# Attention sinks moved into the score bank, head halves summed by loads, two weight sums in one operation

## The chip, the cores and the metric

One core of a Trainium2 chip runs the kernel. The metric is device time in microseconds (us). A smaller number is better. PE is the matrix engine, PEld its weight loads, DVE the vector engine, ACT the activation engine, POOL the general engine, SP the engine that only issues transfers.

## What is computed

One layer of a block with two branches, on a sequence of 2048 positions and 1024 channels, in float32:

```python
h = rms_norm(x, norm_g)
v_c, b_c, c_c, z_c, q, k, v, z_a, gate_logits = split(h @ w_in)
y_a = ((b_c * causal_conv3(c_c * v_c)) * silu(z_c)) @ w_conv_out
o   = sliding_window_attention(rms_norm(q), rms_norm(k), v, sinks) * silu(z_a)
y_b = o @ w_attn_out
merged = sigmoid(g_a) * y_a + sigmoid(g_b) * y_b
out = x + merged @ w_out
```

The attention has 16 query heads and 4 key heads of 64 channels, blocks of 128 queries and a window of 128 keys. Each head has a learned sink, a score that has no value behind it:

```python
m = maximum(max(scores, axis=-1), sink)
p = exp(scores - m)
p = p / (sum(p, axis=-1) + exp(sink - m))
```

## The kernel before

The sequence is worked in two tiles of T = 1024 positions. Nearly all matrix work is a fast form of block multiplication: seven products in place of eight for each pair of column blocks, the "units" of `sunit`, with float32 numbers split into a high and a low part (three matmuls of 128 x 512 for each chunk). A unit of weights `w..._raw` is loaded whole, four sums of its blocks are formed on DVE (`pieces_of`, `sums`), and ACT and DVE split blocks and sums into high (`_ah`, `_sh`, `_th`, `_d`) and low parts. The products gather in the PSUM banks `X`, `V` and `Y`; ACT copies between them (`Y<-X...`, L658).

The program is a list of steps ("ticks"). Each tick is one product of 12 matmuls on PE, about 2.7 us. `run` takes one product, and then all that tables of numbers have put at this tick (`put(n, f)`): forming weights, normalizing, attention. The order in which the Python code writes instructions is the order on each engine; each engine runs its list strictly in that order, except that transfers run beside it once issued. `vec` is DVE with a list of small chains (`Woven`): after each of its operations one waiting step of a chain is written.

Attention is cut into 64 blocks: tile t, key head j, block b of 128 queries, with 4 heads each. `attention` puts the stages of a block at ticks around its step n:

- n - 5: loads of queries and keys (SP)
- n: scores, `att_scores`. Six matmuls fill the one score buffer `s` (`ps_s`, two PSUM banks, 2 x 2 heads of 256 columns of which 192 are used): for each half h one of 384 columns (`s<-lows,kq`, L1236) and two of 192 (`s<-kq,q`, L1240). Then on DVE the mask, the maximum, and the small operations on `st` (128 x 4) for the maximum with the sink. `rq` holds the query factors, which are applied as the scale of the exponential
- n + 1: `att_exp`. ACT takes the exponential of the sink (L1262) and of the four heads (L1265), with their sums
- n + 2: `att_norm` and `att_flip` on DVE (`p<-p,st`, `f<-p`), and the store of `f` by POOL
- n + 4, 9, 10: the way back through memory (`x<-fd`), and the high and low parts `xh`, `xl`, `yp`, cut to the window by POOL
- n + 13: `att_values`, six matmuls of 256 columns into `po`
- n + 14, 15: `att_out`, two copies on ACT that bring one half of `po` to the other 64 partitions, and `att_sum`, two additions on DVE, then the store to `od`

When a tile's units for q, conv, gates are done, the units z and za follow. In `fin_z` the attention result `od` is loaded again (`zain<-od`, four loads a unit, SP) and multiplied by the gate `zas` on DVE. These products become the operands of the output projection.

Three parts of the order matter below. The first: `att_exp` ends at tick n + 1 and steps are at least 3 ticks apart, so the buffer `s` stands free in the tick n - 1. The second: ACT's list holds, beside attention, the copies of `Y` and `s5` and the casts of weight parts that need DVE's sums. The third: POOL's queue holds the transfers with an addition, among them `mt<-tha` (L1551), which add into memory.

Of the kernel before, what the change touches and what calls it, by code (L numbers as in the profile page):

```python
# [82 lines left out]
Z_AHEAD = (7, 4)  # L83
SUM_WAIT = 5
VALUES_LATER = ((0, 10), (0, 30))
EARLY_LOADS = ((0, 29), (0, 30), (0, 31))
# [39 lines left out]
def block_kernel(  # L126
# [22 lines left out]
    upool = ctx.enter_context(tc.tile_pool(name="upool", bufs=2))  # L149
    small = ctx.enter_context(tc.tile_pool(name="small", bufs=12))  # L150
    ps_x = ctx.enter_context(tc.tile_pool(name="ps_x", bufs=2, space=bass.MemoryType.PSUM))
# [66 lines left out]
    sink_r = cols[:, C_S:NC].rearrange("p (j h c) -> p j h c", h=2, c=2)  # L218
    nsink_r = consts.tile([P, NKV, 2, 2], F32, name="nsink_r")
    gqk = consts.tile([P, 1], F32, name="gqk")  # L220
# [7 lines left out]
    def prep_cols():  # L228
        nc.vector.tensor_scalar(
            out=gqk, in0=cols[:, C_Q : C_Q + 1], scalar1=cols[:, C_K : C_K + 1],  # L230
            scalar2=HD ** -0.5, op0=ALU.mult, op1=ALU.mult)
        nc.vector.tensor_scalar(
            out=hbias, in0=cols[:, C_B:C_Q], scalar1=0.5, scalar2=None, op0=ALU.mult)
        nc.vector.tensor_scalar(
            out=nsink_r, in0=sink_r, scalar1=-1.0, scalar2=None, op0=ALU.mult)

# [223 lines left out]
    def pieces_of(n):  # L460
# [37 lines left out]
        if kind in "SP":  # L498
# [508 lines left out]

    rqs = {}

# [13 lines left out]
    def fin_q(t, j):  # L1023
# [58 lines left out]
        def by_query(r):  # L1082

            rq = consts.tile([P, 2, HB, 2, 2], F32, tag="rq", bufs=4, name=f"rq{t}_{j}")
            if not by_pe:
                vec.tensor_copy(rq, r.rearrange("p (c q b h) -> p q b h c", c=2, q=2, h=2))
                rqs[t, j] = rq
# [5 lines left out]
            rqs[t, j] = rq  # L1093

# [131 lines left out]

    def att_scores(t, j, b, ld):
# [4 lines left out]
        sp = ps_s.tile([P, 2, 2, 2 * P], F32, tag="s", name=f"s{nm}")  # L1232
        for h in range(2):
            skip = (2 - h) * HD if first else 0
            keys = slice(h * HD + skip, (h + 3) * HD)
            nc.tensor.matmul(  # L1236
                sp[:, h, :, skip : 3 * HD], lhsT=kq[:, 1, h * P : (h + 1) * P], rhs=kz[:, :, keys],
                start=True, stop=False)
            for c in range(2):
                nc.tensor.matmul(  # L1240
                    sp[:, h, c, skip : 3 * HD], lhsT=q2[:, h, c, :], rhs=kq[:, 0, keys],
                    start=False, stop=c == 1)
        sg = sp.rearrange("p h c k -> p (h c) k")
# [5 lines left out]
        else:  # L1249
            vec.copy_predicated(sg[:, :, 2 * HD : 3 * HD], m, sg[:, :, 0:HD])  # L1250
        st = small.tile([P, 6, G], F32, tag="st", name=f"st{nm}")
        vec.tensor_reduce(out=st[:, 0], in_=sg[:, :, HD : 3 * HD], axis=AX.X, op=ALU.max)
        mul(st[:, 5].rearrange("p (h c) -> p h c", c=2), st[:, 0].rearrange("p (h c) -> p h c", c=2), rv)
        vec.scalar_tensor_tensor(
            out=st[:, 1], in0=st[:, 5], scalar=-1.0, in1=nsink_r[:, j].rearrange("p h c -> p (h c)"),
            op0=ALU.mult, op1=ALU.min)
        add(st[:, 2], sink_r[:, j].rearrange("p h c -> p (h c)"), st[:, 1])
        return sg, st, rv

    def att_exp(t, j, b, got):  # L1260
        sg, st, rv = got
        nc.scalar.activation(out=st[:, 3], in_=st[:, 2], func=AF.Exp)  # L1262
        p = slot([P, G, P], F32, f"p{t}_{j}_{b}")
        for i in range(G):
            nc.scalar.activation(  # L1265
                out=p[:, i, :], in_=sg[:, i, HD : 3 * HD], func=AF.Exp, bias=st[:, 1, i : i + 1],
                scale=rv[:, i // 2, i % 2 : i % 2 + 1], accum_out=st[:, 4, i : i + 1])
        return p, st
# [66 lines left out]
    def att_out(t, j, b, po):  # L1335
        pov = po.rearrange("p (h e s c q) -> p h e s c q", h=2, e=2, s=2, c=2)
        o = slot([P, 2, P], F32, f"o{t}_{j}_{b}")
        parts = []
        for e in range(2):
            own, oth = HALVES[e], HALVES[1 - e]  # L1340
            ov = o[own].rearrange("p c (h s q) -> p h s c q", h=2, s=2)
            nc.scalar.copy(ov, pov[oth, :, e])  # L1342
            parts.append((ov, pov[own, :, e]))
        return o, parts
# [77 lines left out]
    def fin_z(t, j, src, nm, use):  # L1422
        other = {}

        def load():
            for i, q in ((0, 0), (1, 1), (0, 1), (1, 0)):
                o = slot([P, H], F32, f"{nm}in{t}_{j}_{i}_{q}")
                nc.sync.dma_start(o, src[2 * j + i, :, hs(q)])
                other[i, q] = o

        def fin(i, q, val):
# [433 lines left out]
    def attention(t, places):  # L1865
        for r, n in enumerate(places):
# [19 lines left out]
            put(n + late + O_ + 1, step("z", lambda g, j=j, b=b: att_out(t, j, b, g["o"])))  # L1886
            put(n + late + S_, step("t", lambda g, j=j, b=b: att_sum(t, j, b, g["z"])))

# [55 lines left out]
    for t in range(NT):  # L1944
# [34 lines left out]

        zs = [("z", j) + fin_z(t, j, yd[t], "z", use_o) for j in range(NJ)]  # L1980
        zs += [("za", j) + fin_z(t, j, od[t], "za", use_y) for j in range(NJ)]
        zs[0][3]()
# [156 lines left out]
```

## Time and profile before

| | us |
|---|---|
| three runs | 1901.31, 1899.99, 1901.0 (median 1901.0) |
| the profiled execution, its time | 1900.13 |
| the profiled execution, its span | 1898.4 |
| busy PE, PEld | 1888.9, 1572.3 |
| busy DVE, ACT, POOL | 1547.3, 986.6, 590.5 |

The profile shows one execution. Its span, from the first to the last instruction, is 1.7 us less than its time. The granted TensorE clock is 1.0 throughout. A row of a group gives line, engine, operation, output and inputs, shape and count, then busy us and mean ns of one, then the engine's idle time just before and what ended it. A row of a timeline gives start in us, duration in us, engine, line, operation, names, and in brackets the idle time before it. DVE operations that go through the helper all stand at L278 and are told apart by their names. A matmul lasts longer in the profile (0.39 us for 512 columns) than the next one waits to start, since matmuls overlap; the distance of starts is what counts.

### The profile page before, as it was taken

What the parts mean: (1) busy time and instruction counts of PE and PEld (TensorE: products, weight loads), DVE (VectorE), ACT (ScalarE), POOL (GpSimd) and SP (SyncE); (2) the same over time, 40 slices, a digit from 0 to 9 for tenths busy, and PEclk for the clock granted to TensorE, in tenths of its full rate; (3) what the DMA queues carried; (4) which work ended last, traced back from release to release, by engine and by line L of the source; (5) the groups of instructions that cost most, each with busy time, mean ns of one, the idle gap of its engine ahead of it and who ended that gap; (6) DMA issues with size and microseconds to landing.
All of it is one profiled execution on the core that took longest, in us unless ns stands there. A gap on an engine that the chain in (4) does not pass through costs nothing.

```text
span 1898.4 us, 27426 instructions
## 1 busy us (share of the span) xinstructions
PE 1888.9 (100%) x8670; PEld 1572.3 (83%) x8670; DVE 1547.3 (82%) x2620; ACT 986.6 (52%) x1967; POOL 590.5 (31%) x846
## 2 busy tenths in 40 slices
PE   9999999999999999999999999999999999999999
PEld 7888888888888888888888888888888888888887
DVE  7988898898888767669799899888888777787754
ACT  7665455456666443434565545556666434444321
POOL 2073335335655000011462344445556000121000
PEclk9999999999999999999999999999999999999999
DMA  8286555558777857894584655567788887779653
GB/s 294 80 239 178 166 159 171 172 183 248 240 237 230 301 195 247 281 279 113 170 229 118 193 165 152 168 200 234 235 247 270 300 280 267 274 193 269 212 176 111
DMA packets 222497, 402.22 MB, mean 212 GB/s; under 512 B 30032, under 2 KB 104784, under 8 KB 212880
## 3 DMA queue, kind: packets, MB, share of 16 engines
q1 hardware_dynamic: 188224, 313.10, 50.4%
q0 software_dynamic: 30528, 78.94, 16.0%
q10 hardware_dynamic: 3600, 8.42, 1.3%
q8 instruction: 69, 1.13, 0.2%
q14 instruction: 76, 0.62, 0.1%
HBM read 271.09 MB, written 129.25 MB: 211 GB/s over the span
## 4 chain that ended last, share of the span: by engine, by line
PE 89%; DVE 5%; DMA 2%; ACT 2%; issue 1%; SPq 0%; POOL 0%; DVEq 0%; ACTq 0%; POOLq 0%
PE Y L640 33%; PE Xcv L640 4%; PE Vcv L640 4%; PE ya L1468 4%; PE Vq L640 2%; PE Xq L640 2%; PE Xyb L640 2%; PE Vyb L640 2%; PE Vo L640 2%; PE Xo L640 2%; PE Vza L640 2%; PE Xza L640 2%; PE po L1330 2%; PE Xgb L640 2%; PE Vgb L640 2%; PE Xga L640 2%
## 5 line engine op out<-in xcount | busy, mean ns | idle before, releaser
L1292 POOL DMA_DIRECT2D x<-fd x256 | 139.6, 552 | 128.8 <-DMA fd<-f 55.6
L1265 ACT ACTIVATE p<-s,st,rq 128x128 f32<-128x128 f32 x256 | 113.0, 450 | 0.1
L1313 POOL TENSOR_SCALAR_AFFINE_SELECT xh<-xh 64x512 fp32r<-64x512 f32 x64 | 59.3, 927 | 152.7 <-DVE xl L278 103.7
L1285 POOL DMA_DIRECT2D fd<-f x64 | 36.9, 577 | 209.4 <-DVE f L278 173.4
L1551 POOL DMA_DIRECT2D mt<-tha x16 | 13.8, 862 | 255.0 <-DVE tha L278 233.4
L640 PE MATMUL Xcv<-oph,wcv_ah 128*128 128x512 f32 x256 | 79.2, 390 | 0.0
L1313 POOL TENSOR_SCALAR_AFFINE_SELECT xl<-xl 64x512 fp32r<-64x512 f32 x64 | 66.2, 1034 | 4.4
L1313 POOL TENSOR_SCALAR_AFFINE_SELECT yp<-xl 64x512 fp32r<-64x512 f32 x64 | 58.2, 909 | 3.1
L1313 POOL TENSOR_SCALAR_AFFINE_SELECT yp<-yp 64x512 fp32r<-64x512 f32 x64 | 57.4, 898 | 4.2
L278 DVE SCALAR_TENSOR_TENSOR y<-u,cols,y 128x512 f32<-128x512 f32 x64 | 53.3, 834 | 3.8 <-ACT y L1379 2.7
L278 DVE TENSOR_TENSOR o<-po,o 64x256 f32<-64x256 f32 x128 | 53.4, 417 | 2.7 <-ACT o L1342 1.7
L640 PEld LDWEIGHTS Xcv<-oph,wcv_ah 128*128 128x128 f32 x256 | 47.6, 188 | 9.6
L278 DVE TENSOR_TENSOR p<-p,st 128x512 f32<-128x512 f32 x64 | 50.5, 790 | 3.3
L469 ACT CAST wcv_sh<-wcv_raw 128x1024 fp32r<-128x1024 f32 x16 | 16.8, 1051 | 69.7 <-DVE wcv_raw L278 69.7
L1265 ACT ACTIVATION_READ_ACCUMULATOR p<-s,st,rq 128x1 f32 x256 | 50.7, 198 | 0.0
L1342 ACT COPY o<-po 64x256 f32<-64x256 f32 x128 | 47.1, 368 | 6.2 <-DMA wpd_yb<-wph_yb 3.0
L1070 POOL DMA_DIRECT2D q2d<-q_h x64 | 44.2, 690 | 18.1 <-ACT q_h L1065 9.2
L640 PE MATMUL Xcv<-oph,wcv_al 128*128 128x512 f32 x128 | 49.8, 389 | 0.0
L2040 POOL DMA_DIRECT2D oc<-ocd x12 | 6.5, 543 | 136.0 <-DMA wyb_sh<-wpd_yb 119.7
L1070 POOL DMA_DIRECT2D q2d<-q_l x64 | 44.1, 689 | 13.7 <-DMA q2d<-q_h 5.0
L278 DVE TENSOR_TENSOR wcv_raw<-wcv_raw 128x512 f32<-128x512 f32 x64 | 47.3, 758 | 1.1
L278 DVE STREAM_TRANSPOSE f<-p 128x512 f32<-128x512 f32 x64 | 45.5, 711 | 2.9 <-DVE p L278 0.2
(713 smaller groups left out, 6457.9 us busy)
## 6 DMA issues: line engine op xcount, KB each, us to landing
gd<-th SPq DMA_DIRECT2D x64, 256.0 KB, 2.7
wcv_raw<-in_w_units SPq DMA_DIRECT2D x16, 1024.0 KB, 5.4
q<-q2d SPq DMA_DIRECT2D x64, 256.0 KB, 5.4
v<-vd SPq DMA_DIRECT2D x128, 128.0 KB, 3.5
fd<-f POOLq DMA_DIRECT2D x64, 256.0 KB, 4.4
x<-fd POOLq DMA_DIRECT2D x256, 64.0 KB, 3.2
th<-gd SPq DMA_DIRECT2D x48, 256.0 KB, 4.9
wga_raw<-in_w_units SPq DMA_DIRECT2D x8, 1024.0 KB, 5.3
```

The source lines that it names most:

```text
L278: r = f(*args, **kw)
L469: return (lambda: nc.scalar.copy(hi, src), lambda: vec.tensor_tensor(out=lo, in0=src, in1=hi.bitcast(F32), op=ALU.subtract))
L640: nc.tensor.matmul(ps, lhsT=w[:, j, :], rhs=b[:, m, :], start=start and j == 0 and i == 0, stop=j == KP - 1 and i == 2, skip_group_check=n ...
L1070: nc.gpsimd.dma_start(q2d[t][j][half, q * 2 * HB : (q + 1) * 2 * HB, i, e, :], src[HALVES[e]].bitcast(F32).rearrange("p (b x) -> p b x", x ...
L1265: nc.scalar.activation(out=p[:, i, :], in_=sg[:, i, HD : 3 * HD], func=AF.Exp, bias=st[:, 1, i : i + 1], scale=rv[:, i // 2, i % 2 : i % 2 ...
L1285: nc.gpsimd.dma_start(fd, f)
L1292: nc.gpsimd.dma_start(x[QUADS[k]], src[k])
L1313: nc.gpsimd.affine_select(out=d4, in_=s4, pattern=[[0, 2], [-32 * sg, 2], [0, G], [-sg, 32]], compare_op=ALU.is_gt if prev else ALU.is_ge, ...
L1330: nc.tensor.matmul(po[:, cs], lhsT=v2[:, kind + h, :], rhs=xx[:, :, h * HD : (h + 1) * HD], start=n == h == 0, stop=n == 2 and h == 1)
L1342: nc.scalar.copy(ov, pov[oth, :, e])
L1468: nc.tensor.matmul(ps, lhsT=w[:, j, cs], rhs=o[:, m, :], start=n == 0 and i == 0, stop=n == KC - 1 and i == 2)
L1551: nc.gpsimd.dma_start(mt[t][k, :, hs(q)], m, accum_op=ALU.add)
```

## The change

1. Sinks. `keep_query` divides the sinks by the query factors, once for a tile and key head (a reciprocal and a product on DVE, into the new `sr_` tiles). `att_bank` copies them at tick n - 1 on ACT into column 192 of the four heads in `s` (L1238 of the changed kernel). The maximum on DVE and the exponential on ACT then run over 129 columns in place of 128, so that the sink takes part in both. The separate exponential and three small DVE operations go.
2. Order of scores. For each half the two matmuls of 192 columns come first, and the one of 384 last.
3. Halves. `att_out` copies all 128 partitions of `po` with two operations; `att_store` stores the two halves of the partitions apart, into an `od` of twice the size (two transfers). The two DVE additions go. `fin_z` loads one half as before, and `LOW_AT` = 2 ticks later POOL issues a load of the other half that adds into the same tile.
4. Weight sums. The second pair of block sums is one DVE operation of 1024 columns in place of two of 512.
5. The pool of small tiles is smaller (`small` 12 to 10), which makes room for the wider tiles.

```diff
+LOW_AT = 2
...
-    od = [dram.tile([KC, P, T], F32, name=f"od{t}") for t in range(NT)]
+    od = [dram.tile([2, KC, P, T], F32, name=f"od{t}") for t in range(NT)]
...
-                        lambda: sub(raw[:, 1, 1], raw[:, 1, 1], raw[:, 0, 0]),
-                        lambda: sub(raw[:, 1, 0], raw[:, 1, 0], raw[:, 0, 0])))
+                        lambda: sub(raw[:, 1].rearrange("p h j c -> p h (j c)"),
+                                    raw[:, 1].rearrange("p h j c -> p h (j c)"),
+                                    raw[:, 0, 0].rearrange("p j c -> p (j c)").unsqueeze(1).to_broadcast(
+                                        [P, 2, H]))))
...
+        vec.reciprocal(out=s4, in_=rq.rearrange("p q b h c -> p (q b) (h c)"))
+        mul(s4, s4, sink_r[:, j].rearrange("p h c -> p (h c)").unsqueeze(1).to_broadcast([P, NB, G]))
...
+    def att_bank(t, j, b):
+        sp = ps_s.tile([P, 2, 2, 2 * P], F32, tag="s", name=f"s{t}_{j}_{b}")
+        nc.scalar.copy(sp[:, :, :, 3 * HD : 3 * HD + 1], sinks_of[t, j][:, b // HB, b % HB].unsqueeze(3))
+        return sp
...
-        vec.tensor_reduce(out=st[:, 0], in_=sg[:, :, HD : 3 * HD], axis=AX.X, op=ALU.max)
-        mul(st[:, 5].rearrange("p (h c) -> p h c", c=2), st[:, 0].rearrange("p (h c) -> p h c", c=2), rv)
+        vec.tensor_reduce(out=st[:, 0], in_=sg[:, :, HD : 3 * HD + 1], axis=AX.X, op=ALU.max)
         vec.scalar_tensor_tensor(
-            out=st[:, 1], in0=st[:, 5], scalar=-1.0, in1=nsink_r[:, j].rearrange("p h c -> p (h c)"),
-            op0=ALU.mult, op1=ALU.min)
-        add(st[:, 2], sink_r[:, j].rearrange("p h c -> p (h c)"), st[:, 1])
+            out=st[:, 1], in0=st[:, 0], scalar=-1.0, in1=rv.rearrange("p h c -> p (h c)"),
+            op0=ALU.mult, op1=ALU.mult)
...
-        nc.scalar.activation(out=st[:, 3], in_=st[:, 2], func=AF.Exp)
...
-        add(st[:, 5], st[:, 4], st[:, 3])
-        vec.reciprocal(out=st[:, 0], in_=st[:, 5])
+        vec.reciprocal(out=st[:, 0], in_=st[:, 2])
...
-    def att_sum(t, j, b, got):
-        o, parts = got
-        for ov, pv in parts:
-            add(ov, pv, ov)
-        nc.sync.dma_start(
-            od[t][2 * j : 2 * j + 2, :, b * P : (b + 1) * P].rearrange("c p q -> p c q"), o)
+    def att_store(t, j, b, o):
+        for l, half in enumerate(HALVES):
+            nc.sync.dma_start(
+                od[t][l, 2 * j : 2 * j + 2, :, b * P : (b + 1) * P].rearrange("c (e d) q -> d (c e) q", e=2),
+                o[half].rearrange("d c e q -> d (c e) q"))
...
+                if len(src) > 1:
+                    put(tick[0] + LOW_AT, lambda o=o, i=i, q=q: nc.gpsimd.dma_start(
+                        o, src[1][2 * j + i, :, hs(q)], accum_op=ALU.add))
...
-            put(n, step("s", lambda g, j=j, b=b: att_scores(t, j, b, g["l"])))
+            put(n - 1, step("k", lambda g, j=j, b=b: att_bank(t, j, b)))
+            put(n, step("s", lambda g, j=j, b=b: att_scores(t, j, b, g["l"], g["k"])))
```

The first place is ACT's list before the scores of block 7 of the last key head of tile 0 (`s_3_7`). The names `wz_1_...` are parts of a weight unit, `zs_...` gates, `o_`, `xh_`, `yp_` stages of earlier blocks. Before:

```order
L469 CAST wz_1_sh<-wz_1_raw 128x1024
L1342 COPY o_3_3_6174<-po_3_3_6136 64x4x2x32 x2
L1299 CAST xh_3_4_6177<-x_3_4_6002 128x512
L1300 CAST yp_3_4_6179<-x_3_4_6002 64x512
L1436 ACTIVATE zs_1_1_6134<-zs_1_1_6134 128x512
L1436 ACTIVATE zs_1_0_6195<-Y 128x512
L469 CAST wz_1_th<-wz_1_raw 128x1024
L658 COPY Y<-Xz_1_6229 128x512
```

The same place in the changed kernel:

```order
L467 CAST wz_1_sh<-wz_1_raw 128x1024
L1348 COPY o_3_3_6039<-po_3_3_6003 128x4x2x32 x2
L1308 CAST xh_3_4_6042<-x_3_4_5874 128x512
L1309 CAST yp_3_4_6044<-x_3_4_5874 64x512
L1443 ACTIVATE zs_1_1_6001<-zs_1_1_6001 128x512
L1443 ACTIVATE zs_1_0_6060<-Y 128x512
L467 CAST wz_1_th<-wz_1_raw 128x1024
L1238 COPY s_3_7_6081<-sinks_3_1925 128x4
L658 COPY Y<-Xz_1_6095 128x512
```

The sinks' copy stands behind the cast of `wz_1_th`, and the scores of this block wait for it.

The second place is PE's list at the same scores, between two products of the unit z. Before:

```order
L640 MATMUL Xz_1_6229<-oph_1_3_516,wz_1_al 128x512
L1236 MATMUL s_3_7_6245<-lows_148,kq_3_7_6049 128x2x192
L1240 MATMUL s_3_7_6245<-kq_3_7_6049,q_0_3_7_6047 128x192 x2
L1236 MATMUL s_3_7_6245<-lows_148,kq_3_7_6049 128x2x192
L1240 MATMUL s_3_7_6245<-kq_3_7_6049,q_0_3_7_6047 128x192 x2
L640 MATMUL Vz_1_6260<-oph_5_0_750,wz_1_sh 128x512 x2
```

In the changed kernel:

```order
L640 MATMUL Xz_1_6095<-oph_1_3_514,wz_1_al 128x512
L1250 MATMUL s_3_7_6081<-kq_3_7_5921,q_0_3_7_5919 128x192 x2
L1253 MATMUL s_3_7_6081<-lows_147,kq_3_7_5921 128x2x192
L1250 MATMUL s_3_7_6081<-kq_3_7_5921,q_0_3_7_5919 128x192 x2
L1253 MATMUL s_3_7_6081<-lows_147,kq_3_7_5921 128x2x192
L640 MATMUL Vz_1_6123<-oph_5_0_747,wz_1_sh 128x512 x2
```

The number of matmuls stays, and the group now begins with the narrow ones and ends with a wide one.

The third place is DVE's list at the normalization of the block before, `p_3_6`. Before:

```order
L278 TENSOR_TENSOR wz_1_al<-wz_1_raw,wz_1_ah 128x1024
L278 TENSOR_TENSOR o_3_2_6071<-po_3_2_6028,o_3_2_6071 64x4x2x32 x2
L278 TENSOR_TENSOR wz_1_d<-wz_1_raw,wz_1_d 128x512
L278 TENSOR_TENSOR zs_1_1_6134<-Y,s5z_0_6026 128x512
L278 TENSOR_TENSOR st_3_6_6082<-st_3_6_6082 128x4
L278 RECIPROCAL st_3_6_6082<-st_3_6_6082 128x4
L278 TENSOR_TENSOR p_3_6_6117<-p_3_6_6117,st_3_6_6082 128x512
L278 STREAM_TRANSPOSE f_3_6_6146<-p_3_6_6117 128x512
L278 TENSOR_TENSOR zin_0_0_0_5959<-zin_0_0_0_5959,zs_0_0_6100 128x512
L278 TENSOR_TENSOR wz_1_raw<-wz_1_raw 128x512 x4
```

In the changed kernel:

```order
L276 TENSOR_TENSOR wz_1_al<-wz_1_raw,wz_1_ah 128x1024
L276 TENSOR_TENSOR wz_1_d<-wz_1_raw,wz_1_d 128x512
L276 TENSOR_TENSOR zs_1_1_6001<-Y,s5z_0_5897 128x512
L276 RECIPROCAL st_3_6_5953<-st_3_6_5953 128x4
L276 TENSOR_TENSOR p_3_6_5984<-p_3_6_5984,st_3_6_5953 128x4x128
L276 STREAM_TRANSPOSE f_3_6_6012<-p_3_6_5984 128x512
L276 TENSOR_TENSOR zin_0_0_0_5832<-zin_0_0_0_5832,zs_0_0_5969 128x512
L276 TENSOR_TENSOR wz_1_raw<-wz_1_raw 128x512 x2
L276 TENSOR_TENSOR wz_1_raw<-wz_1_raw 128x1024
```

The additions into `o` and one small operation are gone ahead of the sums of `wz_1_raw`, and the last two sums have become one; the rest keeps its order.

More of the change, by code (lines that the diff above doesn't have):

```diff
@@ L149, in block_kernel @@
     upool = ctx.enter_context(tc.tile_pool(name="upool", bufs=2))
-    small = ctx.enter_context(tc.tile_pool(name="small", bufs=12))
+    small = ctx.enter_context(tc.tile_pool(name="small", bufs=10))
     ps_x = ctx.enter_context(tc.tile_pool(name="ps_x", bufs=2, space=bass.MemoryType.PSUM))
@@ L1006, in head_rms, with keep_query @@
         rsqrt(ms, 32, name, ss, 1.0 / HD, then)
-    rqs = {}
+    rqs, sinks_of = {}, {}
+    def keep_query(t, j, rq):
+        rqs[t, j] = rq
+        sr = sinks_of[t, j] = consts.tile(
+            [P, 2, HB, 2, 2], F32, tag="sr_", bufs=4, name=f"sinks{t}_{j}")
+        s4 = sr.rearrange("p q b h c -> p (q b) (h c)")
+        vec.reciprocal(out=s4, in_=rq.rearrange("p q b h c -> p (q b) (h c)"))
+        mul(s4, s4, sink_r[:, j].rearrange("p h c -> p (h c)").unsqueeze(1).to_broadcast([P, NB, G]))
     def squares_sum(a, name):
@@ L1086, in by_query @@
                 vec.tensor_copy(rq, r.rearrange("p (c q b h) -> p q b h c", c=2, q=2, h=2))
-                rqs[t, j] = rq
+                keep_query(t, j, rq)
                 return
@@ L1092, in by_query @@
                     vec.tensor_copy(rq[HALVES[e], :, :, h, :], rv[HALVES[h], :, :, :, e])
-            rqs[t, j] = rq
+            keep_query(t, j, rq)
         return fin
@@ L1231, in att_scores @@
         rv = rqs[t, j][:, b // HB, b % HB]
-        sp = ps_s.tile([P, 2, 2, 2 * P], F32, tag="s", name=f"s{nm}")
         for h in range(2):
@@ L1241, in att_scores @@
                     sp[:, h, c, skip : 3 * HD], lhsT=q2[:, h, c, :], rhs=kq[:, 0, keys],
-                    start=False, stop=c == 1)
+                    start=c == 0, stop=False)
+            nc.tensor.matmul(
+                sp[:, h, :, skip : 3 * HD], lhsT=kq[:, 1, h * P : (h + 1) * P], rhs=kz[:, :, keys],
+                start=False, stop=True)
         sg = sp.rearrange("p h c k -> p (h c) k")
@@ L1250, in att_scores @@
             vec.copy_predicated(sg[:, :, 2 * HD : 3 * HD], m, sg[:, :, 0:HD])
[L1251 to L1253 removed]
+        st = small.tile([P, 3, G], F32, tag="st", bufs=4, name=f"st{nm}")
+        vec.tensor_reduce(out=st[:, 0], in_=sg[:, :, HD : 3 * HD + 1], axis=AX.X, op=ALU.max)
         vec.scalar_tensor_tensor(
[L1255 to L1257 removed]
+            out=st[:, 1], in0=st[:, 0], scalar=-1.0, in1=rv.rearrange("p h c -> p (h c)"),
+            op0=ALU.mult, op1=ALU.mult)
         return sg, st, rv
@@ L1886, in attention @@
             put(n + late + O_ + 1, step("z", lambda g, j=j, b=b: att_out(t, j, b, g["o"])))
-            put(n + late + S_, step("t", lambda g, j=j, b=b: att_sum(t, j, b, g["z"])))
+            put(n + late + S_, step("t", lambda g, j=j, b=b: att_store(t, j, b, g["z"])))
     def next_tile(t, n0):
@@ L1978, in use_y @@
                 put(tick[0] + USE_WAIT[t], lambda: ca(B_AT[k % 2, q], k // 2)) if USE_WAIT[t] else ca(B_AT[k % 2, q], k // 2)
-        zs = [("z", j) + fin_z(t, j, yd[t], "z", use_o) for j in range(NJ)]
-        zs += [("za", j) + fin_z(t, j, od[t], "za", use_y) for j in range(NJ)]
+        zs = [("z", j) + fin_z(t, j, [yd[t]], "z", use_o) for j in range(NJ)]
+        zs += [("za", j) + fin_z(t, j, [od[t][0], od[t][1]], "za", use_y) for j in range(NJ)]
         zs[0][3]()
```

28 lines of the change are left out of this document (9 added, 19 removed).

## The prediction

> **What bounds the kernel now.** I read the page's busy times first, then PE's waits, then PE's starts in a quiet stretch.
>
> ```profile
> span 1898.4 us, 27426 instructions
> PE 1888.9 (100%) x8670; PEld 1572.3 (83%) x8670; DVE 1547.3 (82%) x2620; ACT 986.6 (52%) x1967; POOL 590.5 (31%) x846
> ```
>
> The reader is to see that PE is busy all the time and DVE four fifths of it. From the chain of waits between 715 and 735 us:
>
> ```profile
> 716.23 2.72 PE Vza L640 x12
> 718.95 2.72 PE Y L640 x12
> ```
>
> A product of 12 matmuls takes 2.72 us when nothing disturbs it, 0.227 us from start to start. PE's own waits, by what ended them:
>
> ```profile
> PE po L1330 <- POOL xl L1313: 0.9, 1, 0.9
> PE Y L640 <- DVE Vb L278: 0.4, 1, 0.4
> PE Y L640 <- DVE vr L278: 0.4, 2, 0.2
> ```
>
> Beside the opening, which the change leaves alone, these are the largest; PE hardly ever waits. So work taken from DVE pays only through waits of this size, and any new wait of PE is paid in full. The profiled execution took 1900.13 us, 1.7 over its span; the median of the runs is 0.9 above it. What a measurement of this kernel can tell from no change is about 0.2%, 3.8 us.
>
> **Work that leaves and arrives beside PE.** From the groups by line:
>
> ```profile
> L278 DVE TENSOR_TENSOR o<-po,o 64x256 f32<-64x256 f32 x128 | 53.4, 417 | 2.7 <-ACT o L1342 1.7
> L278 DVE TENSOR_TENSOR st<-cols,st 128x4 f32<-128x4 f32 x64 | 17.9, 280 | 2.2
> L278 DVE TENSOR_TENSOR st<-st,rq 128x4 f32<-128x4 f32 x64 | 15.9, 248 | 2.1
> L278 DVE TENSOR_TENSOR st<-st 128x4 f32<-128x4 f32 x64 | 13.6, 212 | 15.7 <-ACT p L1265 15.2
> L278 DVE TENSOR_TENSOR wcv_raw<-wcv_raw 128x512 f32<-128x512 f32 x64 | 47.3, 758 | 1.1
> L278 DVE TENSOR_TENSOR wcv_al<-wcv_raw,wcv_ah 128x1024 fp32r<-128x1024 f32 x16 | 19.4, 1213 | 0.1
> L1262 ACT ACTIVATE st<-st 128x4 f32<-128x4 f32 x64 | 13.2, 205 | 50.3 <-DVE st L278 49.6
> L1376 ACT COPY halo<-u 128x2 f32<-128x2 f32 x8 | 1.5, 194 | 0.1
> ```
>
> DVE loses the additions, 53.4 us, and the three small operations, 17.9 + 15.9 + 13.6 = 47.4 us: 101 us. The merged sum should cost what the nearest operation of 1024 columns costs, 1213 ns, in place of two of 758: 0.3 us less for each of the 16 units of that group, and alike in the others. What `keep_query` adds (16 operations on 32 columns) I price by the small rows, some 4 us in all, long before the scores that use it. ACT loses 64 exponentials of 205 ns and gains 64 copies; the copy was not in the trace, and I take the nearest row, 194 ns, with 0.1 and 0.4 us as ends. So ACT's load stays; the copies of `po` move 128 partitions in place of 64 with the same 256 columns, which I cost at nothing. If that were wrong, by at most the 0.4 us of a second pass each, ACT has the room in the mean but not at the places below. None of this is on PE's path as such.
>
> What may end is waits. The two of the `vr` kind and the `Vb` one are DVE running behind; with 1.5 us less for each block I take them out: 0.8 us idle. A start that comes late costs more than the idle time shown, because matmuls overlap, as this wait on ACT shows, which has no idle row at all:
>
> ```profile
> 589.96 0.39 PE L640 MATMUL Vz<-oph,wz_sl 128*128 128x512 f32 x1
> 590.46 0.73 PE L640 MATMUL Y<-oph,wz_sh 128*128 128x512 f32 x2
> ```
>
> Between starts lie 0.50 us in place of 0.227, and the pair lasts 0.73, so its second start comes 0.73 - 0.39 = 0.34 after the first, 0.11 late. So a wait costs 0.39 - 0.23 = 0.16 before any idle time shows and 0.11 behind it: three waits, 0.8 + 3 x 0.27 = **-1.6 us**. Ends: 0 and -1.6. The wait on POOL stays, since its additions' operands come through ACT and POOL, which keep their work.
>
> **The new wait: scores behind the sinks' copy.** Before, the scores needed only the exponentials of the block before, two ticks old. Now they need an ACT copy written one tick earlier, so PE feels how far ACT runs behind. I set the changed order on ACT against the trace: for each of the 64 blocks, when the last ACT instruction ahead of the copy ended, and when PE started the scores. In 60 the copy comes in time or nearly so. Four are late. The first, tile 0's last block, ACT and PE:
>
> ```profile
> 584.73 1.05 ACT L469 CAST wz_sh<-wz_raw 128x1024 fp32r<-128x1024 f32 x1 [1.42 <-DVE wz_raw L278]
> 588.88 1.04 ACT L469 CAST wz_th<-wz_raw 128x1024 fp32r<-128x1024 f32 x1
> 586.61 0.33 PE L1236 MATMUL s<-lows,kq 128*128 128x384 f32 x1
> ```
>
> PE starts these scores at 586.61; the cast ahead of the copy ends at 589.92. ACT's run begins with a wait for DVE's sums. That chain passes the exponentials (one less, 0.2 us) and the normalization on DVE (one small operation less, 0.2), so it starts 0.4 earlier. Copy done: 589.92 - 0.4 + 0.2 = 589.7, a wait of 3.1 us. The wait at 590.46 just quoted (0.27 + 0.11 = 0.4 us) then falls away, since `Y` is copied while PE stands. The second place:
>
> ```profile
> 1317.68 0.69 ACT L1409 ACTIVATE th<-Vga,hbias 128x512 f32<-128x512 f32 x1 [4.67 <-PE Vga L640]
> 1323.15 1.05 ACT L469 CAST wga_th<-wga_raw 128x1024 fp32r<-128x1024 f32 x1
> 1322.87 0.33 PE L1236 MATMUL s<-lows,kq 128*128 128x384 f32 x1
> ```
>
> ACT's run starts from PE here, at 1317.68, so DVE's relief does nothing; the exponential (0.2) and the copy (0.2) cancel: 1324.20 - 1322.87 = 1.3 us. The third and fourth:
>
> ```profile
> 499.47 0.21 ACT L1262 ACTIVATE st<-st 128x4 f32<-128x4 f32 x1 [0.86 <-DVE st L278]
> 502.49 0.62 ACT L1300 CAST yp<-x 64x512 fp32r<-64x512 f32 x1
> 502.11 0.22 PE L1236 MATMUL s<-lows,kq 128*128 128x128 f32 x1
> ...
> 342.81 1.05 ACT L469 CAST wcv_sh<-wcv_raw 128x1024 fp32r<-128x1024 f32 x1 [6.34 <-DVE wcv_raw L278]
> 345.95 1.05 ACT L469 CAST wcv_th<-wcv_raw 128x1024 fp32r<-128x1024 f32 x1
> 346.16 0.33 PE L1236 MATMUL s<-lows,kq 128*128 128x384 f32 x1
> ```
>
> At 502 ACT had waited 0.86 for DVE's small operations, two of which go: 503.11 - 0.86 + 0.2 - 502.11 = 0.3 us. At 346 ACT had waited 6.34 us for DVE's sums; DVE runs without a pause there, so I let it gain about half a block's saving, 0.7: 347.00 - 0.7 + 0.2 - 346.16 = 0.3. I allow 0.2 for all others together. Sum 3.1 + 1.3 + 0.3 + 0.3 + 0.2 = 5.2, four late seconds of 0.11, less the 0.4: **+5.2 us**. Ends: +1 (DVE's relief brings ACT forward everywhere but at 1322) and +8 (no relief anywhere: 3.5, 1.5, 1.2, 1.0, and some of the near ones).
>
> What is queued behind the copy on ACT is the next `Y` copy, at most 0.2 us later, with a whole product of cover. Waiting scores delay only DVE's mask, which then delays the exponentials of the same block.
>
> **The order of the six scores.** A group before, with what follows it, and a group of `po` with what follows it:
>
> ```profile
> 330.97 0.33 PE L1236 MATMUL s<-lows,kq 128*128 128x384 f32 x1
> 331.73 0.66 PE L640 MATMUL Xb<-oph,wb_ah 128*128 128x512 f32 x2
> 334.54 0.39 PE L640 MATMUL Y<-oph,wb_th 128*128 128x512 f32 x1
> ...
> 219.27 0.63 PE L640 MATMUL Vcv<-oph,wcv_sh 128*128 128x512 f32 x2
> 222.02 0.33 PE L1236 MATMUL s<-lows,kq 128*128 128x384 f32 x1
> ```
>
> The group takes 0.76, and the 12 matmuls behind it 2.81 in place of 2.72: narrow matmuls at the end cost 0.09 afterwards. Behind `po`, which ends on 256 columns, they take 2.75, 0.03 too long. So a group that ends on 384 should cost less than 0.03 afterwards; I take 0.015. A wide matmul behind a narrow one starts the next about 0.03 later, and the new order has one more of these. Gain 0.09 - 0.015 - 0.03 = 0.045, for the 46 blocks that stand alone, and nearly nothing where `po` comes first: **-2.0 us**. Ends: -4 (no loss at all) and +1.7 (only the 0.03 is paid, 60 times).
>
> Against that stands a rule. The Trainium skill, "TensorE: Matmul & The Clock Gate", section "LDWEIGHTS (loading the stationary operand)", gives a weight load of 128 columns 107 ns whatever follows, and the same page pulls loads ahead of running matmuls. An estimate by it is 4 x 107 + 2 x 163 = 0.75 us for the group in either order, near the 0.76 measured, and nothing for the order: the sum would be 2.0 us higher. It has no place for the 0.09 behind the group, which the trace shows, so I stay with the rows.
>
> **Stores and adding loads.** 64 more stores and 32 more loads move 17 MB more. POOL's part, from the groups, the transfers and the stretch in which the loads fall:
>
> ```profile
> L1551 POOL DMA_DIRECT2D mt<-tha x16 | 13.8, 862 | 255.0 <-DVE tha L278 233.4
> zain<-od SPq DMA_DIRECT2D x32, 256.0 KB, 5.2
> mt<-tha POOLq DMA_DIRECT2D x16, 256.0 KB, 5.4
> L1428 SPq DMA_DIRECT2D zain<-od x32: 319/432/1532, 636.7 to 1565.1; - x32
> L278 DVE TENSOR_TENSOR zain<-zain,zas x32: 680/684/686, 659.8 to 1592.8; 128x512 f32<-128x512 f32 x32
> 650.00:800.00 150.00, 150.00 (x664) 124.17 (x663) 108.74 (x160) 66.13 (x106) 0.00 (x0) 1.00 0.71 240
> ```
>
> The nearest adding transfer takes 0.86 us of POOL and lands after 5.4. POOL does nothing at all in that stretch (0.00), and the last cut of the window stands ahead of these loads in its queue. A load at 636.7 is first used at 659.8, 23 us on. The chain is 5.2 or 2 ticks (5.4), 4 x 0.86 of issue, 5.4 to land: 14 us, 9 to spare. SP has two short issues in place of one, and waits for ACT's copies a tick old in place of DVE's additions. I cost it at 0; without that cover DVE would wait at the head of its queue and PE a product later.
>
> Sum: -1.6 + 5.2 - 2.0 = **+1.6 us** on 1900.13, 1901.7. As the median stands 0.9 higher, I say 1902.
>
> **Rivals.**
> - Order without effect, the rule's result, by rows: the 0.09 stays and the 0.03 cancels against something: +3.6 us, 1904. For it: the tail may come from the group, not its end.
> - Slower: ACT is as late as in the trace. Its place is the copy before the scores; the price +8, waits of 1.6 gone or not, order -2: +5 to +8, 1906 to 1909. It decides once the copies are late by over 7.5 us together. For it: ACT's waits for PE (1317.68) and its casts don't change. Against: 50 us of its waits were for DVE.
> - Faster: DVE's 101 us bring ACT forward, copies late +1, waits gone -1.6, order -4: -4.6, 1896. For it: the waits of 0.86, 1.42 and 6.34 us for DVE ahead of three of the four places. Against: in two of them the chain is ACT's and PE's.
> - Adding loads late: over 9 us more on the chain, by transfers queued behind others (0.71 busy already). Each unit of za then stalls PE by what is over; two us in four units, +8.
> - The store and sum side is hidden anyway: that is the forecast.
>
> **How the numbers follow.** Forecast 0.40 (1898 to 1904); order without effect 0.18 (1902 to 1905, a quarter of it over the bound); slower 0.22; faster 0.15; late loads 0.05. Within 0.2% of 1901.0 means 1897.2 to 1904.8: 0.40 + 0.13 + a little of the faster case, 0.55. Slower 0.22 + 0.05 + 0.04 = 0.31, faster 0.14. The range leaves out half of the faster and a third of the slower case: 1896.5 to 1908.
>
> **What would show it.** PE's waits should name an ACT copy, L1238, at some four scores, 3 us of it in the last block of tile 0; the 12 matmuls behind a group of scores should take under 2.75; `Vb` and `vr` should be gone from PE's waits, and DVE's busy time near 1440. I am wrong if the copies' waits are below 1 us or above 8, if a transfer ends a wait of DVE on `zain`, or if PE waits for the longer sum.

## The result, and the profile after

The changed kernel takes 1919.28 us (median of 5 runs, 1917.62 to 1920.40), the kernel before 1901.0 beside it: a ratio of 1.0095, 95% interval 1.0081 to 1.0110. It is 18 us slower; the prediction said 1902 and no more than 1908. The page of the profile after, its span and busy times:

```profile
span 1918.4 us, 27262 instructions
PE 1894.9 (99%) x8670; PEld 1576.1 (82%) x8670; DVE 1444.8 (75%) x2236; ACT 971.4 (51%) x1967; POOL 637.7 (33%) x878
```

DVE did get down to where the prediction put it (1547.3 before, near 1440 forecast), and the kernel still got 20.0 us longer by the span. PE's waits after, largest first but for the opening (total, times, longest):

```profile
PE Y L640 <- DVE Vza L276: 5.3, 1, 5.3
PE s L1250 <- ACT s L1238: 4.4, 5, 1.4
PE Y L640 <- DVE Vz L276: 3.4, 1, 3.4
PE po L1339 <- POOL xl L1322: 2.4, 3, 1.2
```

The second row is the wait that the prediction gave 5.2 us. The first and the third are two single stops, on results of DVE, whose load had fallen. For the kernels in the table, most of which the experiments below explain, I worked out from the traces how much later each matmul starts than the median for its pair of forms, and summed it by place (us; "all else" holds the opening too, and the last column is from PE's first start to its last):

| kernel | stop in the z stage | stop in the za stage | scores late | `po` late | all else | first to last |
|---|---|---|---|---|---|---|
| before | 0.1 | 0 | 0 | 1.1 | 12.5 | 1892.6 |
| after | 5.2 | 8.0 | 5.6 | 4.5 | 10.6 | 1912.6 |
| e1 sinks alone | 6.8 | 0 | 7.4 | 0.4 | 12.2 | 1905.6 |
| e2 halves alone | 0.1 | 7.5 | 0 | 1.4 | 12.1 | 1900.0 |
| e4 without halves | 5.8 | 0 | 6.8 | 0.7 | 11.9 | 1903.9 |
| f1 later load | 0.1 | 7.7 | 5.2 | 4.5 | 12.2 | 1908.7 |
| f2 earlier copy | 6.9 | 8.1 | 0 | 2.5 | 8.9 | 1905.0 |
| f3 plain second loads | 6.6 | 1.6 | 4.7 | 4.0 | 12.0 | 1907.4 |
| f4 no halves, both mends | 0.1 | 0 | 0 | 1.7 | 11.3 | 1891.7 |
| g1 halves, both mends | 0.9 | 7.0 | 0 | 3.6 | 10.2 | 1900.1 |
| g2 g1, column sum later | 1.8 | 5.5 | 0 | 2.7 | 11.3 | 1899.6 |

**The stop in the z stage.** Before, two issues in this order on POOL and SP (start, duration), POOL's and DVE's operations around them, and how long those transfers took from issue to landing:

```profile
565.30 0.76 POOL L1313 TENSOR_SCALAR_AFFINE_SELECT xl<-xl 64x512 fp32r<-64x512 f32 x1
566.02 0.58 POOL L1285 DMA_DIRECT2D fd<-f  x1
567.62 0.33 SPq L440 DMA_DIRECT2D wz_raw<-in_w_units  x1
...
566.37 1.22 DVE L278 TENSOR_TENSOR wz_tl<-wz_raw,wz_th 128x1024 fp32r<-128x1024 f32 x1
570.66 0.69 DVE L278 TENSOR_TENSOR xl<-x,xh 128x512 fp32r<-128x512 f32 x1 [2.31 <-ACT s5z L667]
...
fd<-f POOLq DMA_DIRECT2D x1, 256.0 KB, 4.6
wz_raw<-in_w_units SPq DMA_DIRECT2D x1, 1024.0 KB, 8.4
```

The same after:

```profile
564.28 1.69 POOL L1322 TENSOR_SCALAR_AFFINE_SELECT xl<-xl 64x512 fp32r<-64x512 f32 x1
565.37 0.33 SPq L438 DMA_DIRECT2D wz_raw<-in_w_units  x1
565.93 0.58 POOL L1294 DMA_DIRECT2D fd<-f  x1
...
wz_raw<-in_w_units SPq DMA_DIRECT2D x1, 1024.0 KB, 9.3
fd<-f POOLq DMA_DIRECT2D x1, 256.0 KB, 8.7
...
564.13 1.21 DVE L276 TENSOR_TENSOR wz_tl<-wz_raw,wz_th 128x1024 fp32r<-128x1024 f32 x1
574.69 0.69 DVE L276 TENSOR_TENSOR xl<-x,xh 128x512 fp32r<-128x512 f32 x1 [9.35 <-issue]
```

The order has turned round. The weight load waits for DVE to be done with the raw buffer (`wz_tl`). DVE reached that operation at 566.37 before and reaches it at 564.13 now, so the 1 MB load goes out 2.2 us sooner, 0.56 ahead of the store of `f` in place of 1.6 behind it.

DVE is only half of the reason, for the store did not keep pace. Counted from the start of the last `xl` on DVE ahead of these operations (561.74 before, 560.50 after), `wz_tl` starts 3.63 us later in place of 4.63: small operations on `st` are gone, and `p` takes 0.69 us in place of 1.10. The store goes out 5.43 us later in place of 4.28: POOL, which issues it behind its cuts to the window, takes 1.30 and 1.69 us for those of `xh` and `xl` in place of 0.76 each (another takes 0.33 less). The load gained 1.0 us and the store lost 1.15, and either alone would have left the store ahead. Both shifts are in every kernel here with the sinks' part and in none without it. Why POOL's cuts take longer is not shown.

The store then lands 8.7 us after its issue, not 4.6. DVE's `xl` starts 0.08 us behind that landing (565.93 + 8.68 = 574.61), and so it does in all thirteen traces: it waits for the store (`f` and `xl` take their buffers from one pool), though the profile names ACT in the one row and nothing (`issue`) in the other as what ended the wait. `Vz`, which PE needs, stands behind `xl` on DVE. The Trainium skill, "DMA: Bandwidth & Descriptors", section "Issuing engines are not separate DMA queues", says that transfers issued by SP, ACT and GpSimd run on the same 16 engines; the trace agrees, since a load issued by SP held up a store issued by POOL.

**The stop in the za stage.** DVE's queue after, with what ended its pauses, PE beside it, and the transfers issued between 1545.5 and 1549.6 (median issue to landing); the last row is `cr` at the like place before:

```profile
1549.66 0.69 DVE L276 TENSOR_TENSOR cr<-cr,cr 128x512 f32<-128x512 f32 x1 [3.95 <-DMA cr<-ocd]
1558.36 1.29 DVE L276 TENSOR_TENSOR cr<-cr,cr 128x512 f32<-128x512 f32 x2 [4.46 <-DMA cr<-ocd]
1559.57 0.69 DVE L276 TENSOR_TENSOR Vza<-s5za,Y 128x512 f32<-128x512 f32 x1
...
1560.31 1.22 PE L640 MATMUL Y<-oph,wza_th 128*128 128x512 f32 x2 [5.27 <-DVE Vza L276]
...
cr<-ocd SPq DMA_DIRECT2D x5, 256.0 KB, 10.0
zain<-od POOLq DMA_DIRECT2D x4, 256.0 KB, 8.7
...
cr<-ocd SPq DMA_DIRECT2D x4, 256.0 KB, 5.0
```

No wait of DVE in this trace ends with an accumulating load. But the loads of `cr`, the z result for the column sums of tile 1, were issued among them and took 10 us in place of 5. DVE's subtraction of them stands ahead of `Vza`, and PE stood 5.3 us. The windows by stage say how full the transfers were (before, then after; the last columns are PE's granted clock, the transfers' busy share and GB/s), and what the stop did to PE behind it:

```profile
1500.00:1600.00 100.00, 99.75 (x441) 82.27 (x440) 73.32 (x107) 38.16 (x61) 0.58 (x1) 1.00 0.80 277
1500.00:1600.00 100.00, 94.73 (x407) 77.94 (x406) 69.75 (x95) 35.16 (x53) 13.94 (x16) 0.97 0.98 302
1560.40:1564.50 4.10, 4.10 (x10) 3.27 (x11) 3.39 (x5) 0.00 (x0) 0.00 (x0) 0.50 1.02 400
```

Busy share 0.98 in place of 0.80: full. In the third row PE ran at a granted clock of 0.50 after its pause, 0.427 us from start to start in place of 0.227, for 11 matmuls: 2.2 us more.

### The profile page after: what moved, and what is told of

Read it like the earlier page. It is cut to its first block, busy times and chain, and to the rows that moved or that the text cites. A ratio compares the mean times of both kernels' runs of the same rounds, so it can differ in the third digit from the quotient of the medians.

```text
span 1918.4 us, 27262 instructions
## 1 busy us (share of the span) xinstructions
PE 1894.9 (99%) x8670; PEld 1576.1 (82%) x8670; DVE 1444.8 (75%) x2236; ACT 971.4 (51%) x1967; POOL 637.7 (33%) x878
## 4 chain that ended last, share of the span: by engine, by line
PE 58%; DMA 5%; DVE 2%; issue 1%; POOL 1%; ACT 1%; SPq 1%; DVEq 0%; POOLq 0%; ACTq 0%
PE Y L640 20%; PE ya L1475 5%; PE Vcv L640 2%; PE Xcv L640 2%; PE Xyb L640 2%; PE Vyb L640 2%; PE Vo L640 2%; PE Xo L640 2%; PE Vza L640 1%; PE Xza L640 1%; PE Vq L640 1%; PE Xq L640 1%; DMA ocd<-zin 1%; PE po L1339 1%; PE Xb L640 1%
## 5 line engine op out<-in xcount | busy, mean ns | idle before, releaser
L1275 ACT ACTIVATE p<-s,st,rq 128x129 f32<-128x129 f32 x256 | 114.2, 461 | 40.0 <-DVE st L276 20.0
L1435 POOL DMA_DIRECT2D zain<-od x32 | 28.0, 1106 | 157.3 <-DMA zain<-od 74.3
L1322 POOL TENSOR_SCALAR_AFFINE_SELECT yp<-xl 64x512 fp32r<-64x512 f32 x64 | 72.5, 1133 | 3.1
L1322 POOL TENSOR_SCALAR_AFFINE_SELECT xl<-xl 64x512 fp32r<-64x512 f32 x64 | 70.1, 1095 | 4.4
L276 DVE TENSOR_TENSOR xl<-x,xh 128x512 fp32r<-128x512 f32 x64 | 44.0, 687 | 15.7 <-issue 9.3
L1250 PEld LDWEIGHTS s<-kq,q 128*128 128x128 f32 x256 | 45.6, 189 | 11.1 <-ACT s L1238 7.8
L1250 PE MATMUL s<-kq,q 128*128 128x192 f32 (+2 forms) x256 | 47.1, 266 | 4.6 <-ACT s L1238 4.4
```

Source lines behind the costliest of these rows:

```text
L276: r = f(*args, **kw)
L1250: nc.tensor.matmul(sp[:, h, c, skip : 3 * HD], lhsT=q2[:, h, c, :], rhs=kq[:, 0, keys], start=c == 0, stop=False)
L1275: nc.scalar.activation(out=p[:, i, :], in_=sg[:, i, HD : 3 * HD + 1], func=AF.Exp, bias=st[:, 1, i : i + 1], scale=rv[:, i // 2, i % 2 : i ...
L1322: nc.gpsimd.affine_select(out=d4, in_=s4, pattern=[[0, 2], [-32 * sg, 2], [0, G], [-sg, 32]], compare_op=ALU.is_gt if prev else ALU.is_ge, ...
L1435: put(tick[0] + LOW_AT, lambda o=o, i=i, q=q: nc.gpsimd.dma_start(o, src[1][2 * j + i, :, hs(q)], accum_op=ALU.add))
```

## The experiments

Each ratio is to the kernel before, in shared rounds, with its 95% interval. A difference between two changed kernels is one of their medians, partly from different rounds; the kernel before had medians of 1900.22 to 1901.0 in them, so such a difference is good to about 1 us.

**One part at a time.** e1: the edits of the bank, the scores, the exponentials and `keep_query` alone.

> The kernel before with the sinks as the 193rd column alone (their columns, the bank's copy on ACT, the new order of a score group, the shorter chain to the exponent, ten buffers of the small pool). Theory A (the split stores and the accumulating loads make other transfers land late, and that costs the two long stops of PE in the trace of after, 8.0 us at 1560 and 5.0 us at 578, and the pauses before value groups beside them): +1 to +4 us, 1902 to 1905: +5.2 of waits of PE for the copy of the sinks, -2 for the order within a group, -1.6 for the waits of before that are gone. Theory B (the sinks' part moves DVE and ACT, and the long stops come from that): 1912 to 1920. Theory C (the parts cost little alone and collide together): 1899 to 1906, and the run with halves alone below 1906 as well.

Measured: 1913.15 us, 1.0069 (1.0056 to 1.0081). PE's waits:

```profile
PE s L1247 <- ACT s L1235: 6.0, 9, 1.3
PE Y L637 <- DVE Vz L275: 4.6, 2, 4.2
```

Theory A falls for this half: the stop in the z stage is here without any split store, and this part alone costs 12.9 us (1900.22 before beside it).

e2: the edits of `od`, `att_out`, `att_store` and `fin_z` alone.

> The kernel before with the value result's halves stored apart and added by accumulating loads alone. Theory A: 1912 to 1918, with a stop of PE of several us in each gate stage (near 578 and near 1560) that ends behind DVE work which waited for a transfer. Theory B: 1900 to 1903. Theory C: below 1906.

Measured: 1907.49 us, 1.0038 (1.0026 to 1.0051). PE waits for `Vza`, and DVE for `cr`, as after:

```profile
PE Y L641 <- DVE Vza L279: 5.2, 1, 5.2
DVE cr L279 <- DMA cr<-ocd: 11.8, 4, 4.6
```

The stop in the za stage belongs to the halves, and there is none in the z stage. So neither A (1912 to 1918 here) nor B holds: each part brings a stop of its own.

e3: the merged sum alone.

```diff
-                        lambda: sub(raw[:, 1, 1], raw[:, 1, 1], raw[:, 0, 0]),
-                        lambda: sub(raw[:, 1, 0], raw[:, 1, 0], raw[:, 0, 0])))
+                        lambda: sub(raw[:, 1].rearrange("p h j c -> p h (j c)"),
+                                    raw[:, 1].rearrange("p h j c -> p h (j c)"),
...
```

> The kernel before with two weight block sums in one operation alone. All theories: 1899 to 1903, no change beyond 2 us, since DVE is not the engine that ends PE's waits there; a change of more than 4 us would show that the order of DVE alone moves PE's stops.

Measured: 1901.11 us, 1.0004 (0.9995 to 1.0013): no change, as expected.

e4: everything but the halves.

> The changed kernel without the halves: sinks and merged sums, with the value result added on DVE and stored in one piece as before. Theory A: 1901 to 1905. Theory B: 1912 to 1920. Theory C: below 1906, and the sum of this run's difference and that of the halves alone well short of +18.

Measured: 1911.70 us, 1.0062 (1.0049 to 1.0074). Theory C falls with it: 11.5 here and 7.3 in e2 make 18.8, about the whole 18.3, so the parts add up. The smaller pool of small tiles (`small`) has no run of its own; it is in e1 and e4, and in f4 below.

**One cause at a time.** f1: the changed kernel with one load moved three rows down in SP's queue, shown here as SP's order.

```diff
- DMA wz_2_raw<-in_w_units 128x2048
  DMA od<-o 64x4x128 x2
  DMA v<-vd 64x512
  DMA v<-vd 64x2x256
+ DMA wz_2_raw<-in_w_units 128x2048
```

> The changed kernel with one weight load (of the third z unit of the first tile, 1 MB) issued behind the two stores of od and the two loads of v of its step instead of ahead of them. Theory D (the stop at 578 is a place in a queue: a faster DVE frees the raw buffer 1.6 us sooner, so the 1 MB load is issued ahead of the store of f that DVE's next operation waits for, and that store lands 9 us after its issue instead of 4.5): the stop of PE there, 3.6 us and the slow matmuls behind it, goes; 1919.3 - 5 = 1914 (1912.5 to 1915.5). Theory E (the stop comes from DVE's and POOL's own order, and the load only stands beside it): 1918 to 1921, the stop stays.

Measured: 1915.78 us, 1.0081 (1.0067 to 1.0095). The transfers issued from 565.2 to 568.6:

```profile
wz_raw<-in_w_units SPq DMA_DIRECT2D x1, 1024.0 KB, 8.7
fd<-f POOLq DMA_DIRECT2D x1, 256.0 KB, 4.6
```

The store lands in 4.6 us again, the stop is gone (5.2 to 0.1 in the table), and theory E falls. By the medians 3.5 us came back and not 5 (3.0 if each is taken against the kernel before in its own rounds; the intervals of the two ratios overlap, so it is the traces that show the stop go). Part of the rest went to the late copy of the sinks at 588.3, where PE stands 1.8 us in place of 1.4 (at 592.7 after), and to half clock behind it, 7 matmuls at 0.2 us more, 1.4 of the 1.6 us that "all else" has grown:

```profile
588.33 0.47 PE L1256 MATMUL s<-kq,q 128*128 128x192 f32 x2 [1.76 <-ACT s L1244]
588.40:591.40 3.00, 3.00 (x12) 2.54 (x13) 3.00 (x3) 0.36 (x1) 2.93 (x4) 0.67 0.86 269
```

f2: the copy behind the previous block's exponentials.

```diff
-            put(n - 1, step("k", lambda g, j=j, b=b: att_bank(t, j, b)))
...
+            def exp(g, r=r, j=j, b=b):
+                e = att_exp(t, j, b, g["s"])
+                if (t, r + 1) in ahead:
+                    ahead[t, r + 1]["k"] = att_bank(t, j, b + 1)
+                return e
```

> The changed kernel with the copy of a block's sinks into its bank put directly behind the exponents of the block before (within a key head; the first block of each head keeps its place). Theory: the waits of PE for that copy (five of them, 4.4 us, 5.2 with what stands around them) go and nothing takes their place, since the copy's 0.19 us and what it waits for come earlier: 1914 (1913 to 1916). Rival: the copy is only the last of several late ACT operations, and other ACT work (the eviction to Y, the exponents) takes its place: 1917 to 1920.

Measured: 1912.56 us, 1.0065 (1.0052 to 1.0078). No row of PE's waits names the copy any more; the largest left are the two stops:

```profile
PE Y L640 <- DVE Vza L276: 5.2, 1, 5.2
PE Y L640 <- DVE Vz L276: 4.2, 1, 4.2
```

6.7 us came back by the medians, though the stop in the z stage is 1.7 us longer here. The 64 copies are all still there; their place in ACT's queue is what cost 5.6.

f3: the second loads plain.

```diff
-                        o, src[1][2 * j + i, :, hs(q)], accum_op=ALU.add))
+                        o, src[1][2 * j + i, :, hs(q)]))
```

> The changed kernel with the second loads of the halves as plain loads on the same queue: the same bytes, issues and order, but the sum of the two halves is left out. Theory F (an accumulating load of 256 KB holds the transfers about 2.0 us where a plain one takes 0.65 us, as the landings in the trace after stand; that makes the loads of cr late that DVE waits for): the stop at 1560 (5.4 us and the slow matmuls behind it, 8.0 in all) shrinks to under 1 us; 1911 (1909.5 to 1913). Rival G (the second loads and the split stores as such): 1917 to 1920.

Measured: 1911.72 us, 1.0057 (1.0043 to 1.0071). `Vza` and the transfers issued from 1541.5 to 1549:

```profile
PE Y L640 <- DVE Vza L276: 0.2, 1, 0.2
...
cr<-ocd SPq DMA_DIRECT2D x8, 256.0 KB, 6.7
zain<-od POOLq DMA_DIRECT2D x4, 256.0 KB, 6.8
```

With the same number of loads and bytes asked for, and only the sum of the halves left out, the stop shrinks from 8.0 to 1.6 us. That is a little over the 1 that theory F allowed, but the time is within its range, and G falls: it is the accumulating that hurts. Its price in the expectation was read too high. In the traces after and e2, four accumulating loads land 2.0 us apart (1552.26, 1554.24, 1556.26, 1558.28 after), but between each two another transfer of 256 KB lands as well. In f3 four plain `cr` loads land 0.62 to 0.66 apart (1553.03 to 1554.97). So an accumulating load held the transfers about 2.0 - 0.65 = 1.35 us, an estimate, twice a plain one. The trace of f2 bears it out: there the two kinds land in turn, an accumulating load 1.36 to 1.41 us behind the transfer ahead of it, a plain one 0.59 to 0.64.

f4: e4 with the edits of f1 and f2.

> Sinks and merged sums without the halves, with the later weight load and the earlier copy of the sinks together. Theories D and the copy: 1911.7 - 5.8 (the stop at 578) - 5.2 (the waits for the copy) = 1900.7 (1898.5 to 1903). Rival: with those gone the next late engine ends the waits, 1905 to 1910.

Measured: 1898.50 us (11 runs), 0.9991 (0.9982 to 0.9999). Its largest waits of PE beside the opening:

```profile
PE Y L643 <- DVE Vz L276: 0.6, 1, 0.6
PE po L1344 <- DMA kq<-kd: 0.6, 1, 0.6
PE Y L643 <- ACT Y L661: 0.5, 1, 0.5
```

Both stops and the waits for the copy are gone and no wait above 0.6 us came. It is the one version whose interval lies below the kernel before, by 2.0 us, which the interval can just tell from nothing. DVE has 49 us less to do in it (1498.3).

**Do the mends add up, and can the halves be kept?** g1: the changed kernel with the edits of f1 and f2.

> The changed kernel, halves and all, with the later weight load and the earlier copy of the sinks together. If the three causes add up: 1919.3 - 3.5 (the load, as measured) - 6.7 (the copy, as measured) = 1909.1 (1907.5 to 1911), with the stop at 1560 left, 5 us and its slow matmuls. Rival: the two mends meet and share part of their gain, 1911 to 1915.

Measured: 1907.86 us, 1.0038 (1.0025 to 1.0050). They add up; what is left above f4 is the halves' 9.4 us (7.3 alone, in e2).

g2: g1 with the second of the four column sums moved.

```diff
-CSUM_AT = (2, 14, 12, 20)
+CSUM_AT = (2, 16, 12, 20)
```

> The same with one of the four column sums of the second tile (their loads of cr and their subtractions) two ticks later, behind the accumulating loads: the accumulating loads stay as they are, but Vza no longer stands behind DVE work that waits for a load among them. Theory F with DVE's order as the path: the stop at 1560 goes as with plain second loads, 1909.1 - 7.6 = 1901.5 (1900 to 1904). Rival: the accumulating loads make another transfer late that PE needs (zain, the weight load), 1905 to 1910.

Measured: 1909.63 us, 1.0043 (1.0031 to 1.0056): the rival. PE's waits, and DVE's queue:

```profile
PE Y L644 <- DVE zas L277: 3.6, 1, 3.6
PE Y L644 <- DVE Vza L277: 1.4, 1, 1.4
...
1549.71 0.69 DVE L277 TENSOR_TENSOR cr<-cr,cr 128x512 f32<-128x512 f32 x1 [5.03 <-DMA cr<-ocd]
```

PE passes this `Vza` in time at 1543 (the `Vza` row is a later unit's, at 1569), but the moved loads of `cr` now land behind a 1 MB weight load, and DVE stands at them ahead of `zas`, the next result that PE needs. The stop moved one operation on. No version with the halves as fast as f4 was found; one that spreads the accumulating loads over a longer time was not tried.

g3: f4 with the order of before in a score group.

```diff
+            nc.tensor.matmul(
+                sp[:, h, :, skip : 3 * HD], lhsT=kq[:, 1, h * P : (h + 1) * P], rhs=kz[:, :, keys],
+                start=True, stop=False)
             for c in range(2):
                 nc.tensor.matmul(
                     sp[:, h, c, skip : 3 * HD], lhsT=q2[:, h, c, :], rhs=kq[:, 0, keys],
-                    start=c == 0, stop=False)
-            nc.tensor.matmul(
-                sp[:, h, :, skip : 3 * HD], lhsT=kq[:, 1, h * P : (h + 1) * P], rhs=kz[:, :, keys],
-                start=False, stop=True)
+                    start=False, stop=c == 1)
```

> Sinks and merged sums without the halves, with the later weight load and the earlier copy, and with the order of a score group as before (384, 192, 192 in place of 192, 192, 384). The prediction's term: +2.0 us, 1900.5 (1899.3 to 1901.8), with 12 matmuls behind a group at about 0.088 us over their usual distance in place of 0.022. Rival (a weight load is hidden alike in either order): 1898.5, the same as with the new order.

Measured: 1899.99 us (11 runs), 0.9996 (0.9987 to 1.0005), 1.5 over f4, with intervals that overlap. The time is in the forecast range, but the condition named with it is not met, as the groups show. One group and the end of the 12 matmuls behind it, in f4 and in g3:

```profile
440.37 0.36 PE L1255 MATMUL s<-kq,q 128*128 128x192 f32 x2
441.16 0.63 PE L643 MATMUL Y<-oph,wga_th 128*128 128x512 f32 x2
443.68 0.39 PE L643 MATMUL Y<-oph,wga_tl 128*128 128x512 f32 x1
...
440.42 0.34 PE L1254 MATMUL s<-lows,kq 128*128 128x384 f32 x1
441.19 0.65 PE L643 MATMUL Y<-oph,wga_th 128*128 128x512 f32 x2
443.76 0.39 PE L643 MATMUL Y<-oph,wga_tl 128*128 128x512 f32 x1
```

The new order is slower within the group (0.79 against 0.77) and faster behind it: 3.31 in all against 3.34. Over all groups of the two traces the old order loses 0.051 us behind a group, not the 0.088 that the kernel before shows with the same order, and the new one 0.021. With what each loses within the group, that makes about 0.7 us for the order over 46 groups; the rest of the 1.5 is waits or noise.

## Why the prediction was wrong

But for the 3 us in the last block of tile 0, every sign that the prediction named came out: waits for the copy between 1 and 8 us, DVE near 1440, 12 matmuls behind a group in 2.74 us, `Vb` and `vr` gone. The time was 17 us off all the same, since each sign watched a term of the sum, and none watched what the sum had put at nothing.

- **Waits of `Vb` and `vr` gone, -1.6.** Right: neither is among PE's waits after, though small waits for `zs` (0.8, 0.2 before) and `zas` (0.4) came.
- **Scores behind the copy, +5.2.** Right in size (5.6 after, 6.7 back in f2), half right in place. The last block of tile 0 lost 1.5 and not 3.1 us, and three of the five late copies were places in tile 1 that I had allowed 0.2, so that the sum fits is partly luck.
- **Order of the scores, -2.0.** In the groups the size seemed right: from before to f4, group and tail become 0.853 to 0.817 us, 46 groups, 1.7. But g3 shows that only some 0.7 of it is the order; what else in the sinks' part shortens the tail is not settled. The rule that the prediction quotes from the Trainium skill (nothing for the order) was nearer to these 0.7 than my term was. The 107 ns that its estimate took for a weight load is not what the profile shows, 188 ns (L1250, 256 loads, after); but six loads fit into a group of 0.77 us, so they overlap and that row is not their price.
- **Stores and accumulating loads, 0: the first step that failed.** I followed the added loads' own chain (14 us of 23) and found it safe, which it was. I asked who waits for them and not who shares the transfers with them, though the row beside it gave a busy share of 0.71, and 0.80 stood in the stage that stopped. Alone it costs 7.3 us (e2), through `cr`, which the prediction does not name. The rival of late loads had the right size, +8, at the wrong place, and a chance of 0.05.
- **DVE's 101 us: the second, a term that was not there.** I took the relief of DVE as harmless or a gain in every case. With the sinks' part it released a 1 MB load 1.0 us sooner, while POOL, which I had said keeps its work, issued a store 1.15 us later (counted from `xl`, as above); the load passed the store, DVE itself waits for that store next, and the stop cost 5.2 us after and 6.8 in e1. The total is not what decides: e2 takes 52 us off DVE, more than e1's 40, and has no stop there. I had checked what is queued behind the copy on ACT, and nothing of what DVE releases on SP.
- **A pause costs more than its length.** My 0.27 beside the idle time was from a pause too short to show idle time. Behind the two long stops PE ran at half pace, 2.2 and 1.3 us more, which no term of mine had.

The sum, in the table's columns: 5.1 + 8.0 (the two stops) + 5.6 (the copy) + 3.4 (`po`) - 1.9 (all else, where the groups' gain and the removed waits are) = 20.2, against 20.0 from first to last start. The 3.4 on `po`, PE's waits for POOL's cuts, is there only with both parts (0.4 in e1, 1.4 in e2). The prediction let this wait stand as it was; no run here takes apart why it grew.

## What to carry to other kernels

An engine that becomes faster issues, or lets others issue, transfers sooner: list the transfers that its operations release, and see which small store or load they would now overtake that the same engine waits for next. Here 1.6 us lay between the two issues, and 1.0 us on one engine and 1.15 on another used them up. Before adding transfers, read the busy share of the stage they fall in, and look for the loads around them that stand at the head of a queue, not only at who uses the new data. And a copy that a matmul newly depends on belongs directly behind the last work that must precede it, here the exponentials of the block before, which turned 5.6 us of waits into none.

## What the hardware showed that was not expected

- After each of the 11 pauses of PE of 3.4 us and more in these traces it ran at half pace for 6 to 12 matmuls, 0.427 us from start to start. After the 27 pauses between 0.8 and 1.8 us that come after the opening (no pause lies between 1.8 and 3.4) it did so in two (f1 at 588.3, 1.8 us; f3 at 1470.3, 1.2 us). The Trainium skill, "TensorE: Matmul & The Clock Gate", section "Part 1: The HAM clock gate (the "warmup" mystery)", gives half clock after an idle window of about 3.4 us. The long pauses agree with that; the two short ones don't. Counted over the 2.5 us up to the end of each of the 27, these two have the most idle time, 1.76 and 1.88 us (f3's pause follows another of 0.70 us); the next, 1.62 us, was not followed by half pace. That window was chosen with the traces in hand, and no run tested it.
- An accumulating load of 256 KB took about 1.35 us of the full transfers (an estimate from the landings above), a plain one 0.65.
- The old order of a score group lost 0.088 us behind it in the kernel before and 0.051 in g3; this stays open.
